# Attention pieces and recurrence steps on one TensorE: attention one piece ahead, given behind the recurrence's first blocks

## The chip, the cores and the metric

The kernel runs on one core of a Trainium2 chip. The metric is the device time of one execution in microseconds (us); the time of a kernel is the median over its runs. TensorE's clock has two levels, 1.2 and 2.4 GHz; the profile gives the granted clock as a share of the upper one.

## What is computed

Two transformer blocks in sequence on x of 1024 tokens by 1024 features, in float32. Only the first block matters here. Its mixing layer has two branches that read the same normed input and are independent until their outputs are projected, gated and added:

```python
o_a = mla_branch(mla_cols, ...)     # softmax attention, 8 heads, 1024 queries by 1024 keys
o_b = rwkv7_branch(rw_cols, ...)    # a recurrence over tokens, 8 heads, run forward and backward
y_a = o_a @ w_o_l[:MLA_WIDTH]
y_b = o_b @ w_o_l[MLA_WIDTH:]
x = x + (gates[:, :, 0] * y_a + gates[:, :, 1] * y_b) @ w_merge[l]
```

The attention of a head is `softmax((q_nope k_nope + q_rope k_rope) * scale) v`. The recurrence updates a 64 by 64 state per head and token: `state = state * w_t + (state a_t) b_t + v_t k_t`, and reads it with `r_t`. Behind the first block's FFN comes a second block (gated linear attention, a convolution, another FFN).

## The kernel before, in words

The method `body` writes the program stage by stage: projections and the preparation of the recurrence, the preparation of attention's queries and keys, then the stage of this case, in which attention and the recurrence are written interleaved, and then `back`, which begins with the output projections (`mix`, products at L960) and goes on to the FFN and the second block.

The interleaving is done with Python generators. `attention` is a generator that yields after each *piece*: 256 queries of one head, two *sub-blocks* of 128 queries. There are 32 pieces. For a sub-block, `scores` (L698 on) makes two half scores of 128 by 512, each of three products (L723), takes their maximum on VectorE (L724), and an exp on ScalarE (`act`, L174); `weighted` transposes the result in eight pieces of 128 by 128 (L745), splits it in two by ScalarE and VectorE (L748, L749), and after the second sub-block multiplies it with the values in 16 products (L754). The scores of the next sub-block are always written ahead of the weighting of this one. At its first call the generator also writes the loads that every head or the first head needs: the shared key part (`d_kr`, L692), the values (L705), the head's keys (L709) and queries (L710), with their splits by `split` (L187 on ScalarE, L190 on VectorE or GpSimd). The tile `raw` has two buffers, which key part, keys and queries take in turn.

`rwkv_scan` is a generator over 2 x 16 *steps*. A step handles one chunk of 64 tokens in each direction; on TensorE it is L859 (state times inputs), L865, L870 (which gives the next state) and L878 (the output), each waiting for a VectorE or ScalarE operation on the result of the one before. A *block* prepares two steps of one direction: products L812, transposes L825 and products L832, with loads at L801 to L805. The first pair of blocks (one for each direction) is written before the first yield; each further pair is written behind a step of even number and used two steps later. All these draw on few PSUM banks: attention's transposes and the blocks take the three banks `s1` of pool `psB2` in turn, attention's scores the two banks `mm` of `psA2`. A tile that is written later in the program gets a bank when the tile before it in the rotation has been read.

The third generator, `rwkv_out` (in `done`), turns finished recurrence outputs into the branch's output from the second half on (L905 to L926). `early` writes the first weight and operand splits of the output projection behind the stage.

The engines' queues are not in the written order: the program is laid out by a scheduler that weighs the written order, the dependences and the tile buffers. So the order of each engine in the built program has to be looked at. The stage in `body` is at L1648 to L1674.

Of the kernel before, what the change touches and what calls it, by code (L numbers as in the profile page):

```python
# [150 lines left out]
class Prog:  # L151
# [976 lines left out]
    def chain(self, banks, n, tags):  # L1128

        k = {1: 0, 6: 0, 7: 0, 4: 0, 2: 1, 5: 2, 3: 2}[n]  # L1130
        if n in (1, 2, 5):
            banks[k] = self.bank(tags[k])
        return banks[k], n in (1, 2, 5)
# [435 lines left out]
    def body(self):  # L1569
# [3 lines left out]
        with ExitStack() as ctx:  # L1573
# [74 lines left out]
            with pool("at2", 2, side="right") as p2, pool("gn", side="right") as gn, pool("at", side="right") as p1, \  # L1648
                    pool("psA2", 2, space=PS) as psA, pool("psB2", 3, space=PS) as self.psB, pool("psD2", 1, space=PS) as psD:
                self.big = lambda tag: self.t(gn, [P, T], tag, bufs=2 if tag == "fin" else 1)  # L1650
                self.gbank = lambda: [self.t(psA, [P, 512], "mm")]
                self.wlg = self.t(gn, [P, 2, 512], "wlg")
                nc.scalar.dma_start(out=self.wlg, in_=I["wlo"][:, 2:4, :])
                self.ats, self.atp, self.ato = [(psA, "mm")] * 2, [(self.psB, "s1")] * 2, psD
                att = self.attention(p1, p2)
                store = lambda j, x: nc.sync.dma_start(out=self.d_ob[j], in_=x)
                chain = lambda *js: (x for j in js for x in self.rwkv_out(j, store))
                done = iter(())
                with pool("rs") as p3, pool("rs2", 2) as p4, pool("psC2", 1, space=PS) as self.psC:
                    scan = self.rwkv_scan(p3, p4)  # L1660
                    next(scan)
                    for j in range(2):
                        for n in range(NCH):
                            next(scan)
                            next(att, None)
                            if n >= GN0:
                                next(done, None)
                        for _ in done:
                            pass
                        done = chain(2 * j, 2 * j + 1)  # L1670
                for _ in att:
                    pass
                self.U = {n: ctx.enter_context(pool("u" + n, self.SLOTS[n])) for n in ("r", "w", "l", "t")}
                early = self.early()  # L1674
# [19 lines left out]
```

## Time and profile before

| | us |
|---|---|
| median of 3 runs | 3025.65 |
| lowest and highest run | 3020.26, 3030.91 |
| the profiled execution | 3031.49 |
| its span in the profile | 3029.8 |
| TensorE busy | 2947.5 (97%) |
| VectorE busy | 2251.5 (74%) |
| ScalarE busy | 1424.2 (47%) |
| GpSimd busy | 254.7 (8%) |
| mean granted clock of TensorE | 0.982 |

The profile is of one execution, and its times are counted from the start of its span. PE is TensorE, ACT is ScalarE, DVE is VectorE, POOL is GpSimd, SP is the queue that issues most loads. A matmul row's busy time includes overlap with the next, so what follows each other is read from the starts. The stage of this case takes from about 580 to 1116 us of the span.

### The profile page before, as it was taken

What the parts mean: (1) busy time and instruction counts of PE and PEld (TensorE: products, weight loads), DVE (VectorE), ACT (ScalarE), POOL (GpSimd) and SP (SyncE); (2) the same over time, 40 slices, a digit from 0 to 9 for tenths busy, and PEclk for the clock granted to TensorE, in tenths of its full rate; (3) what the DMA queues carried; (4) which work ended last, traced back from release to release, by engine and by line L of the source; (5) the groups of instructions that cost most, each with busy time, mean ns of one, the idle gap of its engine ahead of it and who ended that gap; (6) DMA issues with size and microseconds to landing.
All of it is one profiled execution on the core that took longest, in us unless ns stands there. A gap on an engine that the chain in (4) does not pass through costs nothing.

```text
span 3029.8 us, 42671 instructions
## 1 busy us (share of the span) xinstructions
PE 2947.5 (97%) x16080; PEld 2373.9 (78%) x16080; DVE 2251.5 (74%) x3708; ACT 1424.2 (47%) x2394; POOL 254.7 (8%) x372
## 2 busy tenths in 40 slices
PE   8999999999999989999999999999999999999997
PEld 6777786678888777878888778777778788888886
DVE  6686776477777766578888987966776777778876
ACT  5334435556566454354444544643443433335445
POOL 0000001133333202000000000000000000000000
PEclk9999999899999989999999999999999999999998
DMA  3444544532232245323323553223344233334532
GB/s 140 136 160 138 177 134 137 173 117 79 76 94 68 92 145 199 136 83 118 116 103 102 172 209 132 98 101 114 108 151 153 92 119 111 105 105 174 199 120 82
DMA packets 214142, 383.89 MB, mean 127 GB/s; under 512 B 67168, under 2 KB 113520, under 8 KB 213936
## 3 DMA queue, kind: packets, MB, share of 16 engines
q1 hardware_dynamic: 200768, 363.20, 35.8%
q0 software_dynamic: 3712, 12.59, 1.1%
q10 hardware_dynamic: 9456, 5.38, 0.6%
q8 instruction: 126, 2.06, 0.3%
q14 instruction: 80, 0.66, 0.1%
HBM read 252.65 MB, written 128.45 MB: 126 GB/s over the span
## 4 chain that ended last, share of the span: by engine, by line
PE 52%; DVE 5%; ACT 2%; DMA 2%; issue 1%; SPq 0%; DVEq 0%; ACTq 0%
PE d L1160 21%; PE b L1160 11%; PE d L960 7%; PE d L1275 6%; PE b L1275 4%; DVE x L190 1%; DMA l<-d_m 1%; DVE w L190 1%; ACT x L187 1%; PE b L1483 1%; DVE t L1233 1%; ACT w L187 0%; PE b L1480 0%; DVE k L1050 0%; PE b L1473 0%
## 5 line engine op out<-in xcount | busy, mean ns | idle before, releaser
L1160 PE MATMUL d<-x,w 128*128 128x512 f32 x3120 | 751.8, 394 | 10.7 <-ACT t L1163 6.7
L1160 PEld LDWEIGHTS d<-x,w 128*128 128x128 f32 x3120 | 590.2, 190 | 142.8 <-ACT t L1163 7.8
L187 ACT CAST w<-r 128x512 fp32r<-128x512 f32 (+2 forms) x592 | 365.4, 623 | 538.5 <-PE d L1160 204.3
L190 DVE TENSOR_TENSOR w<-r,w 128x512 fp32r<-128x512 f32 (+2 forms) x592 | 412.9, 704 | 76.4 <-ACT w L187 74.7
L1160 PE MATMUL b<-x,w 128*128 128x512 f32 x1584 | 384.3, 390 | 0.0
L1160 PEld LDWEIGHTS b<-x,w 128*128 128x128 f32 x1584 | 297.4, 188 | 62.6 <-issue 1.0
L1275 PE MATMUL d<-x,w 128*128 128x512 f32 x1056 | 258.9, 393 | 10.6 <-ACT w L187 3.8
L1275 PEld LDWEIGHTS d<-x,w 128*128 128x128 f32 x1056 | 197.5, 189 | 58.6 <-ACT w L187 7.7
L960 PE MATMUL d<-x,w 128*128 128x512 f32 x864 | 199.9, 392 | 1.7 <-ACT w L187 0.9
L1275 PE MATMUL b<-x,w 128*128 128x512 f32 x792 | 195.6, 392 | 0.6 <-DVE t L1233 0.6
L960 PEld LDWEIGHTS d<-x,w 128*128 128x128 f32 x864 | 162.9, 189 | 36.8 <-DVE w L190 1.7
L1275 PEld LDWEIGHTS b<-x,w 128*128 128x128 f32 x792 | 149.2, 189 | 32.6 <-DVE t L1233 1.1
L723 PE MATMUL mm<-kt,q 128*128 128x512 f32 x384 | 122.9, 433 | 10.2 <-ACT pr L174 9.9
L1187 DVE TENSOR_TENSOR t<-t,k 128x1024 f32<-128x1024 f32 (+1 forms) x110 | 122.5, 1114 | 12.6 <-ACT t L174 12.3
L1117 DVE TENSOR_TENSOR r<-r 128x512 f32<-128x512 f32 (+1 forms) x80 | 54.3, 679 | 83.1 <-DMA r<-wu 65.9
L187 ACT CAST x<-l 128x512 fp32r<-128x512 f32 (+1 forms) x165 | 97.9, 640 | 36.4 <-DMA l<-d_m 33.0
L190 DVE TENSOR_TENSOR x<-l,x 128x512 fp32r<-128x512 f32 (+1 forms) x165 | 112.0, 710 | 1.7 <-ACT x L187 1.6
L187 ACT CAST whi<-wraw 128x512 fp32r<-128x512 f32 (+2 forms) x59 | 42.9, 727 | 147.9 <-PE mm L209 63.3
L174 ACT ACTIVATE pr<-mm,st 128x512 f32<-128x512 f32 x128 | 87.0, 686 | 41.7 <-DVE st L726 39.8
L209 PE MATMUL mm<-xhi,whi 128*128 128x512 f32 x304 | 96.4, 396 | 8.9 <-ACT whi L187 8.0
L748 ACT CAST pt<-s 128x512 fp32r<-128x512 f32 x128 | 74.0, 589 | 58.3 <-PE s L745 55.9
L523 PE MATMUL mmf<-xhi,whi 128*128 128x512 f32 x256 | 99.4, 414 | 0.6 <-DVE gu L526 0.6
(358 smaller groups left out, 5052.2 us busy)
## 6 DMA issues: line engine op xcount, KB each, us to landing
l<-d_m SPq DMA_DIRECT2D x66, 512.0 KB, 4.9
d_m<-t SPq DMA_DIRECT2D x110, 256.0 KB, 3.8
r<-wg SPq DMA_DIRECT2D x44, 512.0 KB, 4.5
r<-wu SPq DMA_DIRECT2D x44, 512.0 KB, 3.6
r<-wd SPq DMA_DIRECT2D x32, 512.0 KB, 5.0
r<-w_in SPq DMA_DIRECT2D x24, 512.0 KB, 3.2
d_m<-k SPq DMA_DIRECT2D x44, 256.0 KB, 4.0
wraw<-w_in SPq DMA_DIRECT2D x19, 512.0 KB, 3.8
```

Of the source, the lines that this page charges most:

```text
L174: ins = self.nc.scalar.activation(*a, **k).ins
L187: ins = nc.scalar.copy(hi, src).ins
L190: (lo_eng or nc.gpsimd).tensor_tensor(out=lo, in0=src, in1=hi, op=ALU.subtract)
L209: nc.tensor.matmul(ps[:m, h * 512:(h + 1) * 512], a[:, c:c + m], b[:, h * 512:(h + 1) * 512], start=(k == 0 and n == 0), stop=(k == nk - 1 ...
L523: nc.tensor.matmul(ps[h], a[:, c], b[:, HALF[h]], start=(k == 0 and n == 0), stop=(k == 7 and n == 2))
L723: nc.tensor.matmul(ps, Q[a][:, c], K[b][:, HALF[hf]], start=(n == 0), stop=(n == 2))
L748: nc.scalar.copy(dst[0], t3)
L960: self.nc.tensor.matmul(p[h], a[:, c], b[:, HALF[h]], start=(k == order[0][0] and n == 0), stop=(k == order[-1][-1] and n == 2))
L1117: tt(out=c, in0=c, in1=d, op=ALU.add)
L1160: nc.tensor.matmul(ps, w[:, a], x[k][:, b], start=(opens and k == 0 and i == 0), stop=(k == 3 and i == 2), skip_group_check=True)
L1187: tt = lambda e, o, a, b, op: e.tensor_tensor(out=o, in0=a, in1=b, op=op)
L1275: nc.tensor.matmul(ps, w[:, a], X[k][q][:, b], start=(opens and q == 0 and r == 0), stop=(q == n - 1 and r == 2), skip_group_check=True)
```

## The change

One line is added: attention's generator is advanced once behind the first `next(scan)`, that is, behind the first pair of blocks and ahead of the recurrence's first step. In the loop everything stays: a step, then a piece. The 32nd call in the loop then finds attention at its end.

```diff
@@ -1659,6 +1659,7 @@
                 with pool("rs") as p3, pool("rs2", 2) as p4, pool("psC2", 1, space=PS) as self.psC:
                     scan = self.rwkv_scan(p3, p4)
                     next(scan)
+                    next(att)
                     for j in range(2):
                         for n in range(NCH):
                             next(scan)
```

The first place is TensorE's queue at the stage's start. Names: `c` is a step's bank (c_722, c_754 forward and c_726, c_758 backward in step 0), `mm` a half score, `po` an attention output; L812, L825 and L832 write `s` banks for a block. Before:

```order
L859 MATMUL c_726_4916<-S_718_4886,ar_704_4839 128x128 x2
...
L812 MATMUL s_732_4945<-ar_728_4936,bk_729_4937 128x128
...
L865 MATMUL c_722_4893<-ra_723_4896,y_694_4798 64x64 x4
L865 MATMUL c_726_4916<-ra_727_4919,y_706_4841 64x64 x4
...
L870 MATMUL c_722_4893<-uv_695_4799,tm_701_4826 128x128 x2
...
L870 MATMUL c_726_4916<-uv_707_4842,tm_713_4869 128x128 x2
...
L859 MATMUL c_785_5154<-S_717_4883,ar_692_4796 128x128 x2
...
L859 MATMUL c_790_5187<-S_719_4887,ar_704_4839 128x128 x2
L865 MATMUL c_785_5154<-ra_786_5157,y_694_4798 64x64 x4
L865 MATMUL c_790_5187<-ra_791_5190,y_706_4841 64x64 x4
```

With the change:

```order
L859 MATMUL c_758_5046<-S_750_5016,ar_704_4839 128x128 x2
...
L865 MATMUL c_754_5023<-ra_755_5026,y_694_4798 64x64 x4
L865 MATMUL c_758_5046<-ra_759_5049,y_706_4841 64x64 x4
L870 MATMUL c_754_5023<-uv_695_4799,tm_701_4826 128x128 x2
L870 MATMUL c_758_5046<-uv_707_4842,tm_713_4869 128x128 x2
...
L859 MATMUL c_801_5241<-S_749_5013,ar_692_4796 128x128 x2
L859 MATMUL c_806_5274<-S_751_5017,ar_704_4839 128x128 x2
...
L859 MATMUL c_832_5418<-S_750_5016,ar_772_5109 128x128 x2
L723 MATMUL mm_4910<-kt_718_4884,q_726_4898 128x512
...
L745 MATMUL s_745_4982<-ident_87,pr_4926 128x128 x4
L812 MATMUL s_764_5075<-ar_760_5066,bk_761_5067 128x128
L754 MATMUL po_4989<-pt_716_4882,vs_4895 128x256
```

The second pair of blocks (L812 to `s_732`, later L825 and L832) stood between the products of step 0 and step 1; now steps 0 and 1 follow each other alone, then come attention's first two sub-blocks, and the second pair's first L812 (to `s_764`) stands behind that piece's last transposes (L745 to `s_745`), beside its first L754.

The second place is the SP queue of loads at the same time. Before:

```order
L802 DMA bk_819_5352<-d_bk_59 128x2x256
L802 DMA bk_831_5395<-d_bk_59 128x2x256
L802 DMA bk_898_5737<-d_bk_59 128x2x256
L692 DMA raw_5023<-d_kr_80 64x1024
L705 DMA vt_5036<-d_vt_77 128x8x128
L709 DMA raw_5040<-d_k_79 64x1024
L905 DMA bo_9494<-d_bon_64 128x1024
L910 DMA ggl_9498<-d_gl_76 128x1024
L801 DMA ar_818_5351<-d_ar_58 128x2x256
L802 DMA bk_910_5780<-d_bk_59 128x2x256
L801 DMA ar_830_5394<-d_ar_58 128x2x256
L710 DMA raw_5041<-d_q_78 128x1024
```

With the change:

```order
L802 DMA bk_835_5439<-d_bk_59 128x2x256
L802 DMA bk_847_5482<-d_bk_59 128x2x256
L692 DMA raw_4883<-d_kr_80 64x1024
L705 DMA vt_4896<-d_vt_77 128x8x128
L709 DMA raw_4900<-d_k_79 64x1024
L801 DMA ar_834_5438<-d_ar_58 128x2x256
L801 DMA ar_846_5481<-d_ar_58 128x2x256
L905 DMA bo_9582<-d_bon_64 128x1024
L804 DMA y_836_5440<-d_y_62 64x2x128 x2
L804 DMA y_848_5483<-d_y_62 64x2x128
L710 DMA raw_4901<-d_q_78 128x1024
```

The load of the shared key part (L692) stood behind three loads of `bk` and now stands behind two. The first head's queries (L710) stood ahead of the loads of `y` and now stand behind three of them; the loads for the output part (L905, L910) moved back.

The third place is TensorE's queue at the stage's end, from the recurrence's last product (L878) to the first product of the output projection (L960). Before:

```order
L878 MATMUL c_1951_10892<-uv_1865_10423,g_1869_10441 64x64
L723 MATMUL mm_10672<-kt_756_5026,q_1825_10244 128x512
...
L723 MATMUL mm_10677<-kt_756_5026,q_1825_10244 128x512
...
L723 MATMUL mm_10772<-kt_756_5026,q_1825_10244 128x512
...
L723 MATMUL mm_10777<-kt_756_5026,q_1825_10244 128x512
...
L723 MATMUL mm_10805<-kt_756_5026,q_1825_10244 128x512
...
L723 MATMUL mm_10810<-kt_756_5026,q_1825_10244 128x512
...
L723 MATMUL mm_10925<-kt_756_5026,q_1825_10244 128x512
...
L723 MATMUL mm_10930<-kt_756_5026,q_1825_10244 128x512
...
L960 MATMUL d_11081<-t_11016,w_11009 128x512
```

With the change:

```order
L878 MATMUL c_1963_10962<-uv_1881_10510,g_1885_10528 64x64
L723 MATMUL mm_10759<-kt_720_4886,q_1812_10172 128x512
...
L723 MATMUL mm_10764<-kt_720_4886,q_1812_10172 128x512
...
L754 MATMUL po_10788<-pt_1925_10741,vs_10171 128x256
...
L723 MATMUL mm_10859<-kt_720_4886,q_1812_10172 128x512
...
L723 MATMUL mm_10864<-kt_720_4886,q_1812_10172 128x512
...
L754 MATMUL po_10904<-pt_1949_10874,vs_10171 128x256
...
L960 MATMUL d_11081<-t_11016,w_11009 128x512
```

Between the two there were eight half scores (each the first of three products L723) and are now four; the other four have moved ahead of the last L878.

## Rows read from the trace of the kernel before

**Rows 1.** Windows: stretch, length, busy us of each engine, TensorE's granted clock, DMA share

```profile
590.00:621.00 31.00, 27.34 (x247) 22.70 (x244) 20.76 (x40) 17.11 (x34) 14.71 (x21) 0.89 0.79 240
621.00:660.00 39.00, 35.07 (x274) 28.88 (x273) 27.58 (x66) 21.90 (x56) 10.14 (x16) 0.96 0.24 74
660.00:1080.00 420.00, 417.88 (x3521) 347.40 (x3520) 321.00 (x763) 246.17 (x604) 139.99 (x208) 1.00 0.26 80
1080.00:1116.00 36.00, 26.87 (x133) 22.36 (x132) 23.96 (x51) 20.38 (x45) 4.89 (x6) 0.76 0.55 190
```

**Rows 2.** Timeline of TensorE, 590 to 661: start, length, line, operation, idle before

```profile
590.53 1.16 PE L859 MATMUL c<-S,ar 128*128 128x128 f32 x8
...
592.46 1.02 PE L832 MATMUL s<-uv,g 64*64 64x64 f32 x14
...
594.51 1.14 PE L865 MATMUL c<-ra,y 64*64 64x64 f32 x16
...
598.39 0.71 PE L870 MATMUL c<-uv,tm 128*128 128x128 f32 x4
...
600.92 0.68 PE L878 MATMUL c<-uv,g 128*64 128x64 f32 x8
...
606.74 1.73 PE L865 MATMUL c<-ra,y 64*64 64x64 f32 x16 [2.06 <-DVE ra L861]
608.70 2.08 PE L870 MATMUL c<-uv,tm 128*128 128x128 f32 x8 [0.23 <-ACT ra L867]
610.71 1.97 PE L878 MATMUL c<-uv,g 128*64 128x64 f32 x16
612.61 1.75 PE L859 MATMUL c<-S,ar 128*128 128x128 f32 x8
...
614.95 1.20 PE L723 MATMUL mm<-kt,q 128*128 128x512 f32 x4
...
640.74 1.28 PE L723 MATMUL mm<-kt,q 128*128 128x512 f32 x3 [2.76 <-ACT pr L174]
```

**Rows 3.** Timeline of TensorE, 1060 to 1135, the stage's end

```profile
1081.09 0.68 PE L878 MATMUL c<-uv,g 128*64 128x64 f32 x8
1083.98 0.95 PE L723 MATMUL mm<-kt,q 128*128 128x512 f32 x3 [2.21 <-ACT pr L174]
...
1089.18 0.96 PE L723 MATMUL mm<-kt,q 128*128 128x512 f32 x3
1089.97 0.60 PE L745 MATMUL s<-ident,pr 128*128 128x128 f32 x4
1090.33 1.08 PE L754 MATMUL po<-pt,vs 128*128 128x256 f32 x7
...
1096.00 1.65 PE L723 MATMUL mm<-kt,q 128*128 128x512 f32 x3 [3.25 <-ACT pr L174]
...
1115.58 9.14 PE L960 MATMUL d<-t,w 128*128 128x512 f32 x39
```

**Rows 4.** Timeline of the SP queue: issue time of loads at the start

```profile
592.60 4.47 SPq L802 DMA_DIRECT2D bk<-d_bk  x2
...
597.37 0.47 SPq L692 DMA_DIRECT2D raw<-d_kr  x1
...
606.27 0.33 SPq L710 DMA_DIRECT2D raw<-d_q  x1
...
607.64 2.58 SPq L804 DMA_DIRECT2D y<-d_y  x4
```

**Rows 5.** Timeline of ScalarE and VectorE: splits of key part, queries at the start

```profile
602.80 1.99 ACT L187 CAST kt<-raw 64x1024 fp32r<-64x1024 f32 x2 [4.14 <-DMA raw<-d_kr]
...
603.88 2.36 DVE L190 TENSOR_TENSOR kt<-raw,kt 64x1024 fp32r<-64x1024 f32 x2 [1.53 <-ACT kt L187]
...
612.83 1.05 ACT L187 CAST q<-raw 128x1024 fp32r<-128x1024 f32 x1 [3.40 <-POOL sw L840]
```

**Rows 6.** DMA issues, 585 to 630: KB each, median us to landing

```profile
raw<-d_q SPq DMA_DIRECT2D x3, 512.0 KB, 4.5
```

## The prediction

> **What bounds the kernel.** I read the page's busy table first. TensorE is busy for nearly the whole span (the table above), so a change of order that adds and removes no arithmetic can only win or lose time in which TensorE idles or runs at its lower clock. I then read the windows of the stage that the diff touches, where recurrence and attention share TensorE, from about 590 to 1116 us [rows 1]. In the middle, 660 to 1080 us, TensorE is busy 417.88 of 420 us at a granted clock of 1.00: nothing is to be had there. The losses lie at the two ends. From 590 to 660 us it is idle for 3.7 + 3.9 = 7.6 us, with clocks of 0.89 and 0.96. From 1080 to 1116 us it is idle for 9.1 of 36 us at a clock of 0.76. So I read the TensorE timeline of both ends [rows 2, 3], and for the start also the load queue, the operand splits and the time of a load to its landing [rows 4 to 6], since they decide when attention can begin.
>
> The start in [rows 2]: steps 0 and 1 of the recurrence run from 590.53 to 612.6 us, and between step 0's products stand those of the second pair of blocks. Step 1 has no cover: 2.06 us of idle at 606.74, and its products take 1.73, 2.08, 1.97 and 1.75 us where the same ones take 1.14, 2 x 0.71, 2 x 0.68 and 1.16 at the full clock. Attention's first product is at 614.95. The tail in [rows 3]: the recurrence's last products end at 1081.8, then attention runs alone until 1115.58, with holes of 2.21 and 3.25 us that a softmax exp on ScalarE ends.
>
> **The tail: what the lead takes away.** After the recurrence's last product the order now has two sub-blocks' scores where it had four. So one piece no longer runs alone. Its price alone is a row difference: from 1083.98 to 1096.00, 12.0 us [rows 3]. The work in it at the full clock is four half scores of 0.79 (1089.18 to 1089.97), four sets of four transposes of 0.36 (1089.97 to 1090.33), and 16 output products, 2.5 by 1.08 for seven: 3.2 + 1.4 + 2.5 = 7.1 us. That work is still done, but between steps of the recurrence, where TensorE has no holes. Saved: 12.0 - 7.1 = **4.9 us**. At least the 3.25 us hole of that piece should go (lower end 3.2). The upper end is all the idle time of the tail, 9.1 us. I take 4.9, because the last two sub-blocks stand in the new order exactly as they stood from 1096.00 on.
>
> **The start: what the lead costs.** The s1 banks are handed out in program order. Attention's first piece now stands ahead of the second pair of blocks, takes the banks first, and those blocks fall behind its transposes. So step 0 loses its cover, step 1 stays without, and step 2, which needs the second pair, waits for attention. What that costs, in three parts:
>
> 1. Until attention's first product. Its chain begins with the load of the shared key part. In the load queue that load stood behind three loads of bk, of which the last was held until 597 by the second pair's transposes (592.60 + 4.47, [rows 4]); only two now stand ahead, so it goes out at about 593.0 instead of 597.37. It lands 5.4 us later (597.37 to 602.80), 598.4, and its splits end 3.4 us after that (602.80 to 603.88 + 2.36), 601.9 [rows 5]. The query load needs that buffer, and in the new queue it also stands behind three loads of y that wait for step 1's L865. Step 0's L865 stays at 594.51. From a step's L865 to the next L859 it took 5.9 us (606.74 to 612.61), and that L859 1.75, at the lower clock; 7.6 in all, and some 2.4 less at the full one. So step 1's L865 falls at 599.7 to 602.1, say 601, and three y issues of 0.65 each (2.58 for four, [rows 4]) put the query load at about 603.2. It lands after 4.5 us (median, [rows 6]) to 6.6 us (606.27 to 612.83), is cast in 1.05, and attention's first product comes at 608.7 to 610.8; I take 609.6, against 614.95 before. In 590.5 to 609.6, 19.1 us, TensorE has the rest of the first blocks with step 0's L859 (590.53 to 593.48, 2.95), the other products of two steps (2 x 3.92) and two more L859 (2 x 1.16): 13.1. Lost: 6.0 us.
>
> 2. From there to the second pair's first product. Attention alone takes 5.2 us from one sub-block's scores to the next (1083.98 to 1089.18, [rows 3]); two of these, and 2 x (0.79 + 0.36) to the first output product, are 12.7 us. The work in it is six half scores and four sets of transposes, 6.2. Lost: 6.5 us.
>
> 3. Products at the lower clock behind these holes. The window from 621 to 660 us had a clock of 0.96 [rows 1], which is 8% of 39 us at half speed, 1.6 us lost. I keep 1.6.
>
> Sum 14.1 us. The kernel before lost 7.6 (idle) + 2.45 (step 1's four groups, 7.53 against 5.08) + 1.6 = 11.65 us in the same work. The start costs **2.5 us** more. Ends: 0, if the query load lands as fast as its median and a sub-block's period falls as low as its work (then the holes are those of before), and 9 us, if attention begins no earlier than 614.95 (5.4 later than I take) and all of it runs at the lower clock.
>
> **What else moves.** On the load queue the bonus and gate loads (L905, L910) fall behind the key load; they feed the output part that begins only after half the recurrence, so they cost nothing here. The last recurrence output is stored later relative to attention's end, about 20 us ahead of it instead of 33; the first output-projection products do not read it. The early weight splits now fall behind the last piece's exps on ScalarE and VectorE, under 16 output products. No arithmetic is added. From the second piece on each step has the same cover as before, one piece shifted.
>
> **Sum.** 2.5 - 4.9 = -2.4 us. The profiled execution took 3031.5 us, so it would take 3029.1. It stood 5.8 us above the median of the runs, 3025.65, so the median becomes **3023 us**. About 0.3% of this kernel, 9.1 us, is what a measurement can tell from no change, so I call it no change.
>
> **The rivals.**
>
> *The lower clock takes the whole start.* In [rows 2] the step behind the hole of 2.06 us took 2.45 us longer. Now the holes come from 594 on, one behind the other, and nothing dense stands between them until about 622 us. If both steps and both sub-blocks run at the lower level, step 0 and 1 lose 2.45 each on their path, which puts attention's first product at 612 or later, and the two sub-blocks some 3.3 us: the start costs about 8.5 instead of 2.5, and the run is 8.5 - 4.9 = 3.6 us slower than before, 3029 us. It turns to slower once attention's first product comes after about 612.0. For it speaks the 0.76 of the tail, where attention alone has just such holes; against it that part of a hole is shortened by what the slower products fill. The Trainium skill's page "TensorE: Matmul & The Clock Gate" (Part 1, "What's actually happening") says that throttled is the default state and activity releases it; by that rule this rival would be the case, and 3029 the time, and the trace so far agrees in that a clock of 0.76 to 0.89 stands in just the two windows with holes.
>
> *The start costs nothing.* Attention begins so early that its first piece hides in the holes of steps 0 and 1, and the 2.76 us hole at 640.74 goes as well. Then 4.9 to 9.1 us of the tail are won and up to 5 us of the start: 3012 to 3020 us, some 3016 in the middle. Against it: the query load behind step 1's y loads.
>
> *The regular middle stalls.* In the new order the recurrence has four transposes and a few output products between a step's L865 and L870 in each step. Before, with a like cover, there were 2.1 us of idle in 420 us. If ScalarE's copies come late by 0.4 us in each of 30 steps, 12 us are lost: 3035 us. It decides from a tenth of a microsecond per step on; against it, ScalarE is busy only 246 of 420 us.
>
> *The lead does not last.* If the recurrence caught up in the saturated middle, the tail would be as before and only the start's 2.5 us remain: 3028 us. The order of the tail, two sub-blocks instead of four, speaks against it.
>
> **Chances.** The forecast (small gain) 0.50, the lower clock 0.20, a free start 0.17, the stalling middle 0.08, no lasting lead 0.05. Faster by over 0.3% (below 3016.6) takes most of the free start: 0.15. Slower by over 0.3% (above 3034.7) is the stalling middle and a little of the lower clock: 0.10. The rest, 0.75, is no change. The range reaches from the lower middle of the free start, 3013, to where the stalling middle begins, 3035; it takes in the two ends of start (0 and 9) and tail (3.2 and 9.1), and the 3020.26 to 3030.91 over which runs of one kernel lie.
>
> **What would show it.** Right: TensorE idle from 594 to 622 us at a clock under 0.85, attention's first product at 608.7 to 610.8, the second pair's L812 some 12 us later, no hole near 640, a middle as full as before, and 21 to 23 us from the recurrence's last product to the first L960 instead of 34. Wrong: a middle with less than 99% TensorE, a tail of over 30 us, a first product after 612, or a run outside 3016.6 to 3034.7.

## The result, and where the time went

The changed kernel takes 3052.78 us, the median of four runs (3049.53 to 3057.06). The kernel before took 3026.13 on the same chip (3020.26 to 3030.91). The ratio is 1.0089, with a 95% interval of 1.0073 to 1.0105: about 27 us slower, where 3023.0 (3013 to 3035) was predicted.

The profiled execution of the changed kernel took 3057.06 us, its span is 3055.3. The windows of the stage, to be laid beside [rows 1]:

```profile
590.00:621.00 31.00, 19.56 (x138) 15.17 (x137) 18.11 (x34) 14.85 (x29) 14.35 (x15) 0.75 0.78 224
621.00:660.00 39.00, 37.62 (x295) 30.92 (x294) 27.71 (x67) 20.73 (x51) 6.54 (x12) 0.93 0.15 49
660.00:1080.00 420.00, 405.54 (x3333) 337.70 (x3332) 305.75 (x716) 235.36 (x578) 136.06 (x200) 0.98 0.26 79
1080.00:1116.00 36.00, 36.00 (x293) 28.83 (x291) 27.95 (x66) 17.83 (x45) 7.68 (x14) 1.00 0.12 38
```

The third line is the surprise. Between 660 and 1080 us TensorE idles for 14.5 us, where it idled for 2.1 before, and its granted clock is 0.98 instead of 1.00.

An account of the stage makes this comparable. It runs from the recurrence's first L859 to the first L960 behind attention: 590.53 to 1115.58 before, 589.05 to 1140.67 now. In windows of 4 us, the time lost is the idle time plus the busy time multiplied by one less the granted clock; the rest is work at the full clock. The first 90 us are the first 23 windows, the next 400 us the 100 windows behind them. All in us, from one profiled execution of each kernel:

| | before | now | difference | predicted |
|---|---|---|---|---|
| lost in the first 90 us | 12.1 | 21.8 | +9.7 | +2.5 |
| lost in the next 400 us | 2.9 | 21.1 | +18.2 | 0 |
| lost from there on (the tail) | 15.1 | 10.1 | -5.0 | -4.9 |
| work | 495.0 | 498.6 | +3.6 | 0 |
| stage | 525.0 | 551.6 | +26.6 | -2.4 |

The stage holds the whole difference. The tail came out as predicted. TensorE's timeline at the stage's end, for [rows 3]:

```profile
1119.13 0.68 PE L878 MATMUL c<-uv,g 128*64 128x64 f32 x8
1121.87 0.98 PE L723 MATMUL mm<-kt,q 128*128 128x512 f32 x3 [2.05 <-ACT pr L174]
...
1132.79 1.33 PE L745 MATMUL s<-ident,pr 128*128 128x128 f32 x8 [3.11 <-ACT pr L174]
1136.29 4.30 PE L754 MATMUL po<-pt,vs 128*128 128x256 f32 x16 [2.17 <-ACT pt L748]
...
1140.67 4.59 PE L960 MATMUL d<-t,w 128*128 128x512 f32 x17
```

From the recurrence's last L878 to the first L960 it is 21.5 us instead of 34.5, and the hole of 3.25 us in [rows 3] is gone with its piece.

**The middle.** TensorE's groups by line show whose idle time grew, over 586 to 1141 us. The columns are busy time, mean ns of one, and the idle time before the group with what ended it. Before:

```profile
L865 PE MATMUL c<-ra,y 64*64 64x64 f32 x512 | 46.1, 227 | 2.8 <-DVE ra L861 2.7
```

Now:

```profile
L865 PE MATMUL c<-ra,y 64*64 64x64 f32 x512 | 48.9, 227 | 9.6 <-DVE ra L861 9.6
```

The 9.6 us are mostly five holes, one in each of five heads: 1.79 us before the L865 at 734.84, then 1.74, 1.80, 1.74 and 1.80 at 801.27, 866.19, 931.13 and 996.06. In each case VectorE's `ra` (L861) came late. VectorE's timeline ahead of the first one shows why:

```profile
728.44 0.21 DVE L726 TENSOR_SCALAR st<-st 128x1 f32<-128x1 f32 x1
731.09 1.98 DVE L729 TENSOR_TENSOR st<-st 128x1 f32<-128x1 f32 x1 [2.44 <-ACT pr L174]
733.11 0.16 DVE L730 RECIPROCAL st<-st 128x1 f32<-128x1 f32 x1
733.19 1.27 DVE L818 TENSOR_TENSOR g<-s,gmask 128x512 f32<-128x512 f32 x2
734.38 0.41 DVE L861 TENSOR_TENSOR ra<-c,kv 64x256 f32<-64x256 f32 x1
```

L729 adds two columns of 128 by 1 (the sums of the two exp halves). Here it takes 1.98 us. All its 64 instances, before and now (the three numbers are the shortest, the median and the longest in ns):

```profile
L729 DVE TENSOR_TENSOR st<-st x64: 142/160/1022, 623.3 to 1109.3; 128x1 f32<-128x1 f32 x64
L729 DVE TENSOR_TENSOR st<-st x64: 140/160/1986, 617.4 to 1133.4; 128x1 f32<-128x1 f32 x64
```

GpSimd's timeline at the time of the long one:

```profile
728.37 2.35 POOL L190 TENSOR_TENSOR q<-raw,q 128x1024 fp32r<-128x1024 f32 x1 [1.01 <-ACT q L187]
730.68 2.38 POOL L190 TENSOR_TENSOR kt<-raw,kt 64x1024 fp32r<-64x1024 f32 x1
```

L729 ends at 733.07, GpSimd's split of the next head's keys at 733.06. The five longest L729 (1.98, 1.85, 1.99, 1.85 and 1.99 us) all begin 0.4 to 0.6 us into such a split and last until its end. By the Trainium skill, page "SBUF — State Buffer", section "Who interferes with whom", a VectorE instruction with two inputs in SBUF contends with a GpSimd instruction that reads SBUF, and the loser waits for the whole of the other. The traces agree: of the 128 L729 before and now, each of the 40 that took over 0.25 us ended 0.01 to 0.03 us behind the end of a GpSimd instruction, and none of the 88 shorter ones lies within one. Experiments 1 and 3 below agree too.

In the kernel before, the same two instructions meet too. There L729 begins late in the split. GpSimd's timeline of before:

```profile
725.88 2.37 POOL L190 TENSOR_TENSOR kt<-raw,kt 64x1024 fp32r<-64x1024 f32 x1
728.22 0.60 POOL L892 TENSOR_TENSOR ot<-ot,gn 128x256 f32<-128x256 f32 x1
```

VectorE's timeline of before at that place:

```profile
727.57 0.71 DVE L729 TENSOR_TENSOR st<-st 128x1 f32<-128x1 f32 x1
```

It begins 1.7 us into the split and is held for half a microsecond; TensorE has other work, and no hole follows. In three heads of the kernel before the two meet in this way (1.7 to 2.1 us into the split). The lead changed the phase between attention's heads and the recurrence's steps, and with it when the two instructions meet.

These holes also cost clock behind them. The windows from 732 us on:

```profile
732.00:736.00 4.00, 2.21 (x17) 1.58 (x15) 3.96 (x8) 0.63 (x3) 2.20 (x3) 0.93 0.67 212
736.00:740.00 4.00, 4.00 (x27) 3.82 (x26) 0.69 (x3) 1.76 (x4) 0.61 (x1) 0.50 0.02 4
740.00:744.00 4.00, 4.00 (x31) 3.42 (x31) 2.51 (x6) 1.71 (x5) 0.62 (x1) 0.71 0.32 98
744.00:748.00 4.00, 4.00 (x31) 3.50 (x32) 3.77 (x10) 2.66 (x8) 0.83 (x2) 1.00 0.02 4
```

After 1.8 us of idle, TensorE runs at the lower of its levels for some 6 us, though it is busy throughout: 2.0 and 1.2 us more. This is the dearest of the five holes; behind each of the other four the lower clock costs some 1.7 us. In the account, the middle's 21.1 us are 11.3 of idle and 9.8 of lower clock. Not every hole has this price: those of 2.92 us at 1052.88 in experiment 5 and of 2.76 us at 637.03 in experiment 8 are followed by windows at 1.00.

**The start.** TensorE's timeline, for [rows 2]:

```profile
589.05 1.16 PE L859 MATMUL c<-S,ar 128*128 128x128 f32 x8
...
605.36 0.88 PE L859 MATMUL c<-S,ar 128*128 128x128 f32 x4 [1.85 <-DVE ot L879]
608.56 2.92 PE L723 MATMUL mm<-kt,q 128*128 128x512 f32 x6 [2.33 <-ACT q L187]
616.77 1.65 PE L723 MATMUL mm<-kt,q 128*128 128x512 f32 x3 [5.28 <-ACT pr L174]
...
622.76 1.65 PE L723 MATMUL mm<-kt,q 128*128 128x512 f32 x3 [1.35 <-ACT pr L174]
...
626.83 0.48 PE L812 MATMUL s<-ar,bk 64*128 64x128 f32 x2
```

Attention's first product is at 608.56, where 609.6 was predicted; counted from the first L859 it is 19.5 us, for 19.1. The second pair's first L812 is at 626.83, 18.3 us later. The clock in between:

```profile
608.00:612.00 4.00, 2.92 (x6) 1.82 (x6) 2.46 (x4) 1.73 (x6) 1.52 (x2) 0.50 1.04 289
612.00:616.00 4.00, 0.00 (x0) 0.00 (x0) 0.60 (x2) 1.10 (x2) 0.01 (x1) 0.50 0.84 220
616.00:620.00 4.00, 3.23 (x10) 2.65 (x11) 1.77 (x4) 2.91 (x6) 3.96 (x2) 0.50 0.18 51
620.00:624.00 4.00, 2.65 (x9) 1.85 (x8) 2.51 (x6) 1.94 (x5) 0.78 (x1) 0.50 0.49 171
```

The hole of 5.28 us ends with an exp, and ScalarE's timeline shows what that exp stood behind:

```profile
614.87 1.04 ACT L187 CAST kt<-raw 64x1024 fp32r<-64x1024 f32 x1 [3.63 <-DMA raw<-d_k]
...
615.94 0.69 ACT L174 ACTIVATE pr<-mm,st 128x512 f32<-128x512 f32 x1
```

It is the cast of the second head's keys, which waits for its load ahead of the first head's exp.

### The profile page after: what moved, and what is told of

The parts are those of the page before. It is cut to its first block, busy times and chain, and to the rows that moved or that the text cites. A ratio compares the mean times of both kernels' runs of the same rounds, so it can differ in the third digit from the quotient of the medians.

```text
span 3055.3 us, 42663 instructions
## 1 busy us (share of the span) xinstructions
PE 2956.0 (97%) x16080; PEld 2378.3 (78%) x16080; DVE 2254.8 (74%) x3708; ACT 1422.9 (47%) x2394; POOL 256.3 (8%) x372
## 4 chain that ended last, share of the span: by engine, by line
PE 51%; DVE 5%; ACT 2%; DMA 2%; issue 1%; SPq 0%; DVEq 0%; ACTq 0%
PE d L1160 21%; PE b L1160 11%; PE d L960 7%; PE d L1275 6%; PE b L1275 4%; DVE x L190 1%; DVE w L190 1%; DMA l<-d_m 1%; ACT x L187 1%; PE b L1483 1%; DVE t L1233 1%; ACT w L187 0%; PE b L1480 0%; DVE k L1050 0%; PE b L1473 0%
## 5 line engine op out<-in xcount | busy, mean ns | idle before, releaser
L1160 PE MATMUL d<-x,w 128*128 128x512 f32 x3120 | 750.1, 394 | 12.7 <-ACT t L1163 7.1
L1275 PE MATMUL d<-x,w 128*128 128x512 f32 x1056 | 258.6, 393 | 10.1 <-DVE w L190 3.9
L960 PE MATMUL d<-x,w 128*128 128x512 f32 x864 | 199.5, 391 | 1.7 <-ACT w L187 0.9
L960 PEld LDWEIGHTS d<-x,w 128*128 128x128 f32 x864 | 162.6, 188 | 36.8 <-DVE w L190 1.7
L723 PE MATMUL mm<-kt,q 128*128 128x512 f32 x384 | 120.8, 432 | 12.8 <-ACT pr L174 10.5
L748 ACT CAST pt<-s 128x512 fp32r<-128x512 f32 x128 | 73.3, 589 | 68.3 <-PE s L745 67.9
L749 DVE TENSOR_TENSOR pt<-s,pt 128x512 fp32r<-128x512 f32 x128 | 87.0, 683 | 17.9 <-ACT pt L748 16.7
```

What stands on the lines that cost most here:

```text
L723: nc.tensor.matmul(ps, Q[a][:, c], K[b][:, HALF[hf]], start=(n == 0), stop=(n == 2))
L748: nc.scalar.copy(dst[0], t3)
L749: nc.vector.tensor_tensor(out=dst[1], in0=t3, in1=dst[0], op=ALU.subtract)
L960: self.nc.tensor.matmul(p[h], a[:, c], b[:, HALF[h]], start=(k == order[0][0] and n == 0), stop=(k == order[-1][-1] and n == 2))
L1160: nc.tensor.matmul(ps, w[:, a], x[k][:, b], start=(opens and k == 0 and i == 0), stop=(k == 3 and i == 2), skip_group_check=True)
L1275: nc.tensor.matmul(ps, w[:, a], X[k][q][:, b], start=(opens and q == 0 and r == 0), stop=(q == n - 1 and r == 2), skip_group_check=True)
```

## The experiments

Ratios are against runs of the kernel before on the same chip (medians 3024.27 to 3026.13), with 95% intervals. The stage and its parts are those of the account, from one profile each. The time at which the stage begins differs by up to 8.5 us between executions (first L859 at 582.07 to 590.53 where the order up to it is the same), so the stage says more than the span.

| kernel | us | ratio | stage | first 90 | next 400 | tail | work |
|---|---|---|---|---|---|---|---|
| before | 3026.13 | 1 | 525.0 | 12.1 | 2.9 | 15.1 | 495.0 |
| changed | 3052.78 | 1.0089 (1.0073 to 1.0105) | 551.6 | 21.8 | 21.1 | 10.1 | 498.6 |
| 1 | 3036.99 | 1.0036 (1.0023 to 1.0049) | 533.7 | 20.8 | 2.2 | 11.3 | 499.3 |
| 2 | 3022.36 | 0.9991 (0.9983 to 1.0) | 526.8 | 15.8 | 1.8 | 15.3 | 494.0 |
| 3 | 3038.14 | 1.0043 (1.003 to 1.0056) | 537.6 | 18.9 | 4.3 | 11.4 | 502.8 |
| 4 | 3023.25 | 0.9993 (0.9984 to 1.0002) | 526.7 | 14.5 | 2.1 | 14.6 | 495.4 |
| 5 | 3023.7 | 0.9996 (0.9982 to 1.0009) | 521.5 | 11.5 | 5.0 | 10.1 | 495.0 |
| 6 | 3049.69 | 1.0081 (1.0065 to 1.0097) | 548.9 | 20.2 | 19.7 | 10.5 | 498.6 |
| 7 | 3029.69 | 1.0018 (1.0006 to 1.003) | 531.9 | 20.0 | 2.3 | 10.4 | 499.2 |
| 8 | 3031.7 | 1.0024 (1.0012 to 1.0037) | 528.2 | 13.3 | 5.0 | 11.4 | 498.5 |
| 9 | 3023.67 | 0.9996 (0.9984 to 1.0008) | 527.3 | 16.8 | 4.7 | 12.0 | 493.8 |
| 10 | 3017.76 | 0.9978 (0.9964 to 0.9992) | 520.8 | 10.9 | 3.4 | 11.6 | 495.0 |
| 11 | 3029.58 | 1.0021 (1.0007 to 1.0035) | 531.1 | 17.5 | 5.5 | 9.5 | 498.6 |

### 1 and 2: the sum with one operand in SBUF

```diff
-            nc.vector.tensor_tensor(out=st[:, 5:6], in0=st[:, 3:4], in1=st[:, 4:5], op=ALU.add)
+            nc.vector.reduce_sum(st[:, 5:6], st[:, 3:5], axis=AX.X)
```

Experiment 1 is this edit in the changed kernel, experiment 2 in the kernel before.

> The changed kernel with one edit: the sum of the two halves of the exponentials' sums (L729, 128x1) is a reduction over the two columns, with one operand in SBUF, instead of an addition with two. The order of the instructions on every engine is that of the changed kernel. Theory A: L729 is held by GpSimd's split of the next head's keys (L190, 2.38 us). In the changed kernel it takes 1.85 to 1.99 us instead of 0.16 at 731.09, 797.66, 862.45, 927.52 and 992.31, ends each time when that split ends, and what is queued behind it on VectorE (L730, two L818, then the ra of L861) comes that much later, for which TensorE waits 1.74 to 1.80 us at its first L865. Then L729 takes 0.2 us at those five places, the holes before L865 shrink from 1.8 us to 0.5 or less (0.5 is left if the scaling of bk, L822, still comes late for L825), and the stretches of lower clock behind them (0.50 and 0.71 in the 8 us behind the first) go too: 65 us of a head become 61 to 62.5, five times, so 14 to 20 us: 3033 to 3039 us. Theory B (rival): it is GpSimd's queue, in which the splits stand ahead of the scaling of bk and S (L822, L840), and VectorE only waits for that: then the holes stay over 1.2 us and the time within 4 us of the changed kernel's 3053.

> The kernel before with the same edit of L729. In the kernel before L729 is held too, but by 0.3 to 0.9 us at most and where TensorE has other work (no hole stands behind 727.57, 788.33 or 851.37). Theory A: nothing to be won in the middle: within 3 us of before, 3023 to 3029. Theory C (rival): the two-operand addition costs VectorE more than it shows, and every kernel gains from the edit: 5 us or more faster, under 3021.

Experiment 1 gives 3036.99 us, within theory A's 3033 to 3039. VectorE's timeline at the first of the five places:

```profile
727.63 0.15 DVE L729 TENSOR_REDUCE st<-st 128x1 f32<-128x2 f32 x1 [2.44 <-ACT pr L174]
727.82 0.17 DVE L730 RECIPROCAL st<-st 128x1 f32<-128x1 f32 x1
727.90 1.27 DVE L818 TENSOR_TENSOR g<-s,gmask 128x512 f32<-128x512 f32 x2
729.09 0.41 DVE L861 TENSOR_TENSOR ra<-c,kv 64x256 f32<-64x256 f32 x1
```

GpSimd's split of the keys still runs from 727.22 to 729.60, and L729 now takes 0.15 us inside it. The split, and all instances of L729:

```profile
727.22 2.38 POOL L190 TENSOR_TENSOR kt<-raw,kt 64x1024 fp32r<-64x1024 f32 x1
L729 DVE TENSOR_REDUCE st<-st x64: 135/155/158, 617.7 to 1113.8; 128x1 f32<-128x2 f32 x64
```

TensorE's group for L865:

```profile
L865 PE MATMUL c<-ra,y 64*64 64x64 f32 x512 | 48.9, 227 | 0.8 <-DVE ra L861 0.7
```

The 9.6 us of idle are down to 0.8, and the loss of the middle from 21.1 to 2.2. GpSimd's queue and its instructions are unchanged, so theory B is out. What is left is still 11 us slower than before. Experiment 2 gives 0.9991 (0.9983 to 1.0), 3.7 us by the medians: 3022.36, just below theory A's 3023 to 3029, and the rival's 5 us or more do not show.

### 3: the splits on VectorE

```diff
-                e = nc.gpsimd if h else nc.vector
+                e = nc.vector
```

> The changed kernel with the splits of keys and queries (L190) on VectorE for all heads, as the first head has them, instead of GpSimd for heads 1 to 7. L729 as in the changed kernel. Theories A and B: nothing of 2.4 us stands on GpSimd any more, L729 takes 0.2 us, and the holes of 1.8 us once per head go; VectorE gets 1.8 + 1.2 us per head (the first head's splits at 602.73 and 608.54) in a head of 65 us in which it is busy for 47.5, and may hold ra back by up to those 1.8 us if the order puts a split ahead of it: 3032 to 3045. If neither is right and a new head costs a hole by its loads or casts, the 1.8 us stay and the time is 3050 or more.

3038.14 us. L729 keeps its two operands, and the group for L865 idles as little as in experiment 1:

```profile
L865 PE MATMUL c<-ra,y 64*64 64x64 f32 x512 | 49.2, 227 | 0.8 <-DVE ra L861 0.7
```

So the loss needs both partners, the operation with two operands in SBUF and the long split on GpSimd. Taking either away is enough. L729 did not fall to the expected 0.2 us everywhere: in four heads it takes 1.02 us, until the end of a split of 1.29 us that GpSimd keeps (that of the values), but no hole before L865 follows. The work is the highest of all, 502.8 us; why was not tried.

### 4 and 5: the lead in the tail alone

In the kernel before, with (1, 13) in experiment 4 and (1, 11) in experiment 5:

```diff
                             next(att, None)
+                            if (j, n) == (1, 11):
+                                next(att)
```

> The kernel before in which attention gets its extra piece only behind step 14 of the second half (of 16), so that the start and all but the last steps run as before and only the tail has the lead. The prediction's own term for the tail: 12.0 us alone less 7.1 us of work that moves: 4.9 us faster (3.2 to 9.1), so 3021 us (3017 to 3023). Rival: the last steps can't take the piece, it only moves the end of the recurrence by as much: within 2 us of before.

> The kernel before with attention's extra piece behind step 12 of the second half (of 16); in the run with it two steps later the order behind the recurrence's last product did not change (three pieces stood there, as before), here one piece moves ahead of it. Start and middle as before. The prediction's term for the tail: 12.0 us alone less 7.1 us of work that moves, 4.9 us faster (3.2 to 9.1), so 3021 us (3017 to 3023); the changed kernel and the one with the single operand lie 21.5 and 23.1 us between the recurrence's last product and the first product behind attention, for 34.5, and so this should be 21 to 24 us here. Rival: the recurrence's last steps are held back by as much as the tail gets shorter: within 1.5 us of before.

Experiment 4 is a miss: the extra piece came too late to change the order. The output products of three pieces still stand behind the recurrence's last product, and it is 33.8 us from there to the first L960, as before.

In experiment 5 the piece moved. It is 21.2 us from the last L878 (1088.89) to the first L960 (1110.09), and the tail loses 10.1 instead of 15.1. The prediction's term is there. But the median does not move, 0.9996 (0.9982 to 1.0009). Part of the gain is paid where the piece is put in. TensorE's timeline there, in a hole that an exp ends:

```profile
1052.88 0.97 PE L723 MATMUL mm<-kt,q 128*128 128x512 f32 x3 [2.92 <-ACT pr L174]
```

By the stage 3.5 us are left (521.5 for 525.0), less than these runs can tell from nothing.

### 6 and 7: the second head's cast behind the first exps

```diff
-                self.split(K[0][0:64], K[1][0:64], k[0:64], e)
+                self.split(K[0][0:64], K[1][0:64], k[0:64], e, place["exp"] if h == 1 else None)
...
-                self.act(LNEXP, pr[:, HALF[hf]], ss[hf], AF.Exp, bias=st[:, 2:3], scale=QSCALE, accum_out=st[:, 3 + hf:4 + hf])
+                x = self.act(LNEXP, pr[:, HALF[hf]], ss[hf], AF.Exp, bias=st[:, 2:3], scale=QSCALE, accum_out=st[:, 3 + hf:4 + hf]); place.setdefault("exp", x)
```

Here `act` returns its instruction. Experiment 7 adds the edit of L729.

> The changed kernel with one edit: on ScalarE the cast of the second head's keys (L187, kt) stands behind the first two exponentials (L174, pr) instead of ahead of them. Theory D: the hole of 5.28 us of TensorE at 616.77 is the ScalarE queue standing at that cast until its load lands (idle for 3.63 us until 614.87), with the exponentials ready since L726 at 612.63. Then the first exponential is at 612.7, the product behind it at 613.5, the hole 2.0 us, and what follows comes 2.8 to 3.3 us earlier, with the lower clock behind it perhaps 1 to 2 us more: 3047 to 3050 us. Rival E: the cast only stands in the way one place later (it still waits for the same load, and the first copy of transposed weights, L748, stands behind it): the time moves by less than 1.5 us from 3053.

> The changed kernel with both edits, the cast of the second head's keys behind the first two exponentials and L729 with one operand. If the two losses lie at different places, as the traces say, they add: 3037 less 3 to 5, so 3032 to 3034 us. Not faster than before (3026) in any case, since the start still loses what the missing steps of the recurrence covered before.

3049.69 us falls in theory D's range, but its ratio of 1.0081 (1.0065 to 1.0097) is not clear of the changed kernel's 1.0089 (1.0073 to 1.0105), and the trace speaks for the rival. TensorE's timeline:

```profile
607.98 0.96 PE L723 MATMUL mm<-kt,q 128*128 128x512 f32 x3 [2.02 <-ACT pr L174]
614.84 1.65 PE L723 MATMUL mm<-kt,q 128*128 128x512 f32 x3 [4.33 <-ACT pr L174]
```

The first hole shrank from 5.28 to 2.02 us as expected, and the next grew from 1.35 to 4.33. Together they are 6.35 for 6.63. On ScalarE the cast, and the next head's cast of queries, now stand ahead of the copies of transposed weights (L748):

```profile
609.80 1.04 ACT L187 CAST kt<-raw 64x1024 fp32r<-64x1024 f32 x1 [1.21 <-DMA raw<-d_k]
610.88 1.04 ACT L187 CAST q<-raw 128x1024 fp32r<-128x1024 f32 x1
611.83 1.06 ACT L748 CAST pt<-s 128x512 fp32r<-128x512 f32 x2
```

The first 90 us lose 20.2 for 21.8. The cast in the queue was real, but what it held up is mostly held up by the next thing. Experiment 7 came out better than expected by the median (3029.69 for 3032 to 3034), but its interval overlaps that of experiment 1, and its stage is only 1.8 us shorter. That moving the cast gains anything is not shown.

### 8 and 10: the lead taken later; 9: experiment 5 with one operand

All three are the kernel before with the edit of L729 and the extra piece at (0, 2), (1, 8) and (1, 11).

> The kernel before with L729 on one operand and attention's extra piece behind step 2 of the first half instead of ahead of step 0. Theory F: what is left of the changed kernel's loss (3037 to 3022 with one operand in both) is the start: attention cannot begin before its keys and queries are there, so the lead is got by holding the recurrence back, and at the second piece (L756 at 629.45 for 627.79) the recurrence has done two steps less. With the start as before that loss goes and the tail's gain of 4 us stays: 3016 to 3020 us, faster than both kernels. Rival G: the lead costs wherever it is taken, since the steps of the recurrence that are left alone at some place then lack cover: 3024 us or more.

> The same with the extra piece behind step 9 of the second half, so that one head's splits and blocks lie behind it. If the loss of the kernel with the lead from step 2 (528.2 us for the stage, against 525.0 to 526.8 without) is paid once where the extra piece is put in (2.55 us of idle at 676.41 and a clock of 0.92 around it), this gives the same stage here, 524 to 528 us, and 3023 to 3029; if it is paid in every head behind it (holes of 0.4 to 0.6 at 718, 768, 781 and 844), it is nearer to the last kernel: 520 to 523 us, 3018 to 3023.

> The kernel before with attention's extra piece behind step 12 of the second half and L729 on one operand. From the recurrence's first L859 to the first L960 behind attention, the traces show 525.0 to 526.8 us in the three kernels with the old order up to the tail, 521.5 in the one with the extra piece there. The edit of L729 has little to win with this order (0 to 4 us in its own run): 519 to 522 us for the stage, 3018 to 3023 us for the run, 1 to 8 us faster than before. Rival: the hole that the extra piece made in its place (2.92 us at 1052.88) grows with the other order, and the run is like before, 3024 or more.

Theory F falls. With the start as before (13.3 us lost), experiment 8 is still slower than before: 1.0024 (1.0012 to 1.0037). Its tail wins 3.7 us (11.4 for 15.1), its middle loses 2.1 us more, and its work is 498.5 for 495.0. The time is the rival's, and the lead costs in the stretch behind it; but the rival's reason, steps without cover, can only stand for the middle's 2.1 us, and the larger part is the work, for which it has none.

Experiment 10, with the lead from step 9 of the second half on, is **faster than both kernels**: 0.9978 (0.9964 to 0.9992), some 7 us. Work is 495.0, the tail loses 11.6, and the place where the piece is put in costs 2.4 us of holes on TensorE's timeline:

```profile
1007.04 1.65 PE L723 MATMUL mm<-kt,q 128*128 128x512 f32 x6 [0.64 <-DVE fin L924]
1010.92 0.95 PE L723 MATMUL mm<-kt,q 128*128 128x512 f32 x3 [1.79 <-ACT pr L174]
```

Of the two cases put down for it, this is the one in which the lead is paid for in every head behind it. How much of the 7 us the lead gives is open: experiment 2, the edit of L729 alone, has an interval that overlaps this one. Experiment 9 gives nothing (0.9996, 0.9984 to 1.0008), and its stage of 527.3 misses the 519 to 522 expected. Its start lost 16.8 us, 5.3 more than that of experiment 5 with the same order there; the hole at the extra piece did not grow (2.91 for 2.92 us).

### 11: the second pair of blocks first

In the changed kernel with the edit of L729:

```diff
-        blk, nxt = [None, None], [block(0, 0, 0), block(0, 1, 7)]
+        blk, nxt, two = [None, None], [block(0, 0, 0), block(0, 1, 7)], [block(0, 0, 1), block(0, 1, 6)]
...
-                nxt = [block(jj, 0, step // 2 + 1), block(jj, 1, 6 - step // 2)]
+                nxt = two if jj + step == 0 else [block(jj, 0, step // 2 + 1), block(jj, 1, 6 - step // 2)]
```

> The changed kernel with L729 on one operand and the second pair of the recurrence's blocks written ahead of its first yield, so that the pair stands ahead of attention's extra piece, takes its s1 banks first and covers step 0 as before. Theory H: the start is lost because that pair falls behind attention's first piece. In the first 90 us behind the first L859 the changed kernel loses 21.8 us by idle time and lower clock (before: 12.1), with L729 on one operand 20.8. Then it loses 12 to 15 here, the stage from the first L859 to the first L960 is 525 to 528 us instead of 533.7, and the run 3027 to 3031 us for 3037. Rival I: the start is bound by attention's own chain of loads, splits and exponentials, whatever stands ahead of it, and the pair only moves it back: attention's first product then comes over 25 us behind the first L859 (19.5 in the changed kernel, 24.4 before), the stage stays at 531 or more, the run at 3033 or more.

It lies between the two. By the time, 3029.58, theory H; by the stage, 531.1, and by attention's first product, the rival. TensorE's timeline:

```profile
582.51 1.16 PE L859 MATMUL c<-S,ar 128*128 128x128 f32 x8
...
600.77 1.97 PE L865 MATMUL c<-ra,y 64*64 64x64 f32 x16 [4.49 <-DVE ra L861]
...
610.18 1.20 PE L723 MATMUL mm<-kt,q 128*128 128x512 f32 x4 [1.11 <-ACT q L187]
```

Attention begins 27.7 us behind the first L859, step 0 is covered, and step 1 has a hole of 4.49 us. The first 90 us lose 17.5 for 20.8. So neither theory holds as it was put. That the pair's place is a part of the start's cost is possible but not shown: the intervals of experiments 11 and 1 overlap, and 3.3 us at the start is less than executions of one order differ by (below).

## Why the prediction was wrong

**The step that failed** is the sentence on what else moves: "From the second piece on each step has the same cover as before, one piece shifted", with "nothing is to be had there" on the middle. The middle lost 18.2 us more. I read "full" as "safe": a stage that is full gives nothing back, but it can lose. TensorE's cover was nearly the same; what changed was which VectorE and GpSimd instructions meet. In the trace of before, L729 ran from 142 to 1022 ns, a factor of seven for a sum of 128 by 1. I did not look at it. Experiments 1 and 3 remove the loss from either side.

The sum would have failed without this loss too: experiment 1, without it, is still 11 us slower than before. The start cost more than its 2.5 us, and the work, put at nothing because no arithmetic is added, came to 3.6 us more of TensorE's time.

**The rival of the stalling middle** had the right stretch and 3035 us, with a chance of 0.08, but neither the place nor the mechanism. Its place is the wait for ScalarE's copies before L870, and the idle time there, by the same groups by line, fell from 2.0 to 1.2 us over the stage. It was not copies late by 0.4 us in 30 steps, but one VectorE sum late by 1.8 us in five, which holds back L865, and nearly as much again by the clock behind it, which the rival did not price.

**The tail** was right. Predicted were 4.9 us; the account shows 5.0, and 21.5 us from the last L878 to the first L960 for a forecast of 21 to 23.

**The start** was right in its order and in the wait for the query load, and mis-sized in one term. Until attention's first product 6.0 us of loss were predicted; the holes up to 608.56 add up to 6.1. From there to the second pair 6.5 were predicted, and the holes are 5.28 + 1.35 = 6.6. That sum agrees by luck: the prediction takes two like periods of attention's own chain, and the trace has one long hole behind the cast of the second head's keys, which waits for its load; the prediction has neither. The third term, products at the lower clock, was put at 1.6, the value of before. It measured 5.8 in the first 40 us, since the clock stood at 0.50 from 608 to 624 and every product there took twice as long: 18.3 us to the second pair instead of 12.7. Holes of 3.2 us at the second head (664 to 677) came on top, while the 2.76 us at 640.74 went, as predicted. So the first 90 us cost 9.7 more, just over the upper end of 9. The loss there varies between executions of one order, from 10.9 to 16.8 in the six traces with the old start; against their mean of 13.6, the four with the changed start (changed, 1, 6 and 7: 21.8, 20.8, 20.2, 20.0, mean 20.7) cost 7.1.

**The rival of the lower clock** had that mechanism and nearly that price (8.5), though not its condition: attention's first product did not come after 612.0. That a low clock stands in just the two windows with holes, as it says, passes over the window from 621 to 660 in [rows 1], which idles 3.9 us at 0.96. Its rule from the Trainium skill's page "TensorE: Matmul & The Clock Gate", section "What's actually happening" in Part 1, that activity releases the clock, fits the four windows at 0.50 from 608 to 624 us, in which TensorE is busy for 0 to 3.2 of 4 us. Its 3029 us missed because the middle was left out.

**What stays open.** Work at the full clock is 3.5 to 4.3 us more in six of the seven kernels that have the lead through the middle, and 7.8 in experiment 3, while the six without it keep 493.8 to 495.4. L865 has 2.8 us more busy time for the same 512 products in the changed kernel, but the cause was not tried. The traces give one count that goes with it: how often two matmuls that start one behind the other in the stage come from different lines of the program. It is 815 to 821 in the six without the lead in the middle, 831 to 848 in six of the seven with it, and 859 in experiment 3. That these changes cost the time is not shown. Of the start, experiments 6 and 11 show 1.6 and 3.3 us less, in one profile each, which the spread within one order covers; its cost was not taken apart.

## What to carry to other kernels

Before shifting the phase of two interleaved streams, look for instructions whose longest duration is many times their median: they already meet something, and where they meet it is what the shift changes. On VectorE, keep tiny operations with two SBUF operands out of a queue that the critical path uses while GpSimd runs long instructions; a form with one operand costs the same (155 ns in the median for 160 here). And a stretch in which TensorE is full has next to nothing to gain from a change of order and much to lose: a hole there costs its length, and in the changed kernel nearly as much again by the clock behind it.

## What the hardware showed that I had not expected

A VectorE sum of 128 by 1 took 0.14 to 1.99 us, and the long ones ended with a GpSimd instruction; the same sum with one operand took 0.135 to 0.158 us in all 64 instances of experiment 1, of which 32 lie wholly within a GpSimd instruction. And after a hole of 1.8 us in a stretch of full TensorE, the granted clock was 0.50 and 0.71 in the next two windows of 4 us, although TensorE was busy for all of them, while holes of 2.76 and 2.92 us in experiments 8 and 5 left it at 1.00.
